# Attention scores of two heads in one product of 128 rows, in three rounded parts

## The chip, the cores and the metric

The kernel runs on one core of one Trainium2 chip. What counts is the device time of one execution in microseconds (us), as the median of several runs. The engines work side by side, each through its own instructions in order: TensorE (PE in the rows; its weight loads are PEld), VectorE (DVE), ScalarE (ACT), GpSimd (POOL), and SyncE (SP), which only issues DMAs here.

## What is computed

The reference is a trunk of two layers over 256 tokens of width 1024. In each layer one projection of the normalised input feeds three token mixers: attention with a window of 128 tokens (8 query heads, 2 key heads of 64), a state space branch (S5 with a gated linear unit), and a convolution branch. Their outputs are gated, added and projected onto the residual; a SwiGLU feed-forward block and a gated per-layer embedding follow. The attention scores, which the change touches:

```python
scores = jnp.einsum('bnqkgd,bnjkd->bnkgqj', qb, kb) * (HEAD_DIM ** -0.5)
scores = jnp.where(mask[None, :, None, None], scores, NEG_INF)
m = jnp.maximum(jnp.max(scores, axis=-1, keepdims=True), sink)
pr = jnp.exp(scores - m)
denom = jnp.sum(pr, axis=-1, keepdims=True) + jnp.exp(sink - m)
```

`qb` has 4 query heads (g) for each of 2 key heads (k). All data are float32.

## The kernel before, in words

The 256 tokens are two blocks of 128 (t = 0, 1), which lie on the 128 partitions. Every large matrix product is made by `gemm` (L443): a weight pair of 128 x 1024 is loaded by SyncE, split by ScalarE into a rounded part `wh` (L176, the type float32r) and by VectorE into the rest `wl` (L200), and each product of a float32 matrix is three TensorE products of rounded parts: high x high, high x low, low x high. A buffer of `wh` or `wl` comes free when TensorE has used it, so the splits follow TensorE's pace. `split` (L229) is the helper: a ScalarE copy for the high part, a VectorE subtraction for the low part (with a factor: a scaled copy and one multiply-and-subtract).

The products of a layer stand in a list, `ORDER` (L34): `zk`, `zc`, `zq` project to keys and values with the state space input, convolution input, and queries; `g..` are the gates, `y.` the attention's output projection, `c.` the convolution's, `u.` the gated linear unit's four pieces (u0 and u1 make the left half of the merged tensor `M`, u2 and u3 the right half). Then come `mo` (the mix's output), `fz` and `fo` (feed-forward), `ez` and `pz` (embedding).

Everything else runs as streams, Python generators that are advanced by `pump` (L387) after every six products of a `gemm`. A stream gives its next instructions when a model of the engines' clocks says that their inputs are there; for VectorE, ScalarE and POOL only up to a certain time ahead of TensorE's clock (5.5 us in layer 0's mix, 3.9 in layer 1's). So the order on every engine is fixed when the program is built, by modelled times, and each engine takes it in that order. Streams with a smaller number go first: attention 2, set-up of the state space branch (`ssm_prep`) 3, state space (`ssm_stream`) and convolution (`conv_stream`) 4. In layer 0 `ssm_prep` runs beside the mix: a long chain on POOL, then on VectorE, ScalarE and TensorE, and its last pieces (`kt`, `TJ`) are inputs of the state space branch (`yx`).

`attn_stream` (L830) handles one block: it turns the rotated keys and queries with TensorE (`kTp`, `qTp`), copies them with ScalarE to `kT` (L843) and `qT` (L849, with the factor 0.125), and makes the scores in one or two batches (one of eight heads for block 0, whose window holds 128 keys; two of four heads for block 1 with 256). A batch fills two PSUM banks. In each bank a rounded product with the identity writes the mask (L861), then plain float32 products of 64 rows add the scores (L864): bank 0 takes the heads of key head 0, whose 64 rows are the upper half of the partitions, bank 1 those of key head 1 in the lower half. VectorE takes the row maxima (L871), ScalarE the exponentials (L879). The products with the values (`po`) and the turn back (`oT`) follow. In the profile the tile of the scores is `sc`.

Of the kernel before, what the change touches and what calls it, by code (L numbers as in the profile page):

```python
# [6 lines left out]
F32 = mybir.dt.float32  # L7
F32R = mybir.dt.float32r
# [22 lines left out]
GELU_C = 0.7978845608028654  # L31
GELU_A = 0.044715

ORDER = ["zk zc zq g20 g10 g11 g00 g21 g01 y0 y1 c0 c1 u0 u2 u1 u3".split(),  # L34
         "zk zq zc g01 g11 g10 g00 y0 u0 g20 y1 c0 u2 u1 g21 c1 u3".split()]
AHEAD = 3
NBUF = 4
# [37 lines left out]
def bc(ap, axis, n):  # L75
    a = ap.unsqueeze(axis)
    shape = list(a.shape)
    shape[axis] = n
    return a.broadcast_to(shape)


def trunk_kernel(tc, wts, par, bmat, cst_d, x_d, pos_d, pt_d, bias_d, fg_d, out_d, dbg=None):
# [3 lines left out]
    with ctx:  # L86
# [8 lines left out]
        def b2(shape, dt=F32, name="b2"):  # L95
            return act.tile(shape, dt, tag="b2", bufs=25, name=name)
# [76 lines left out]
        def copy(out, in_, scale=None):  # L173
            if scale is None:
                run("act", 80 + 0.833 * cols(out), [out], [in_])
                ACT.copy(out=out, in_=in_)  # L176
            else:
                func(out, in_, AF.Copy, scale)
# [81 lines left out]
        POOL.memset(mhalf, -0.5)  # L260
        POOL.memset(phalf, 0.5)
        POOL.memset(one1, 1.0)
        mone = cp.tile([128, 8], F32, name="mone")
        POOL.memset(mone, -1.0)
        brow = [cp.tile([128, 512], F32, name=f"brow{i}") for i in range(3)]
# [562 lines left out]
            tt(z2, ra[:, 2], ra[:, 3], ALU.add)  # L828

        def attn_stream(t, S):  # L830
            zqk, vt, kT, par_l = S["zqk"], S["vt"], S["kT"], S["par"]
            nk = 128 * (t + 1)
            hpt = 1024 // nk
            mk = maskr[:, 256 - nk:256]
            z = zqk[t]
            yield lambda: S["rope_ok"]
            yield on_dve(z)
            rope_step(t, z)
            yield on_pe(z)
            zf = z.rearrange("p h d -> p (h d)")  # L840
            pt = p_tr("kTp")
            transpose(pt[:, 0:128], zf[:, 512:640])
            copy(kT[:, 128 * t:128 * t + 128], pt[:, 0:128])  # L843
            S["k_done"] += 1
            pt = p_tr("qTp")
            for k in range(4):
                transpose(pt[:, k * 128:k * 128 + 128], zf[:, k * 128:k * 128 + 128])
            qT = b2([128, 4, 128], name="qT")
            copy(qT.rearrange("p a b -> p (a b)"), pt, 0.125)  # L849
            yield lambda: S["k_done"] > t  # L850
            st = act.tile([128, 6, 8], F32, tag="ast", bufs=4, name="ast")
            sink = par_l[:, O_SINK:O_SINK + 8]
            scs = []
            for b in range(8 // hpt):
                sc = b4([128, hpt, nk], name="sc")
                scs.append(sc)
                yield from sm_units.take(2)
                pts = [p_sm("sc").rearrange("p (i k) -> p i k", k=nk) for _ in range(2)]
                yield on_pe(qT, kT, into=pts)
                for hf in range(2):  # L860
                    mm(pts[hf], identr, bc(mk, 1, hpt // 2), True, False)  # L861
                    rows = slice(64 * hf, 64 * hf + 64)
                    for i in range(hpt // 2):
                        mm(pts[hf][:, i], qT[rows, b * hpt // 2 + i, :],  # L864
                           kT[rows, 128 - nk + 128 * t:128 * t + 128], False, i == hpt // 2 - 1)
                sl = slice(hpt * b, hpt * b + hpt)
                mx = st[:, 0, sl].rearrange("p (i f) -> p f i", f=2)
                for hf in range(2):
                    yield on_dve(pts[hf])
                    run("dve", 615, [st], [pts[hf]])  # L870
                    DVE.reduce_max(out=mx[:, hf], in_=pts[hf], axis=AX.X)  # L871
                yield on_dve(st)
                tt(st[:, 1, sl], st[:, 0, sl], sink[:, sl], ALU.max)
                tt(st[:, 2, sl], sink[:, sl], st[:, 1, sl], ALU.subtract)
                ts(st[:, 1, sl], st[:, 1, sl], -1.0, ALU.mult)
                for i in range(hpt):
                    yield on_act(st)
                    slot = hpt * b + i
                    func(sc[:, i], pts[i % 2][:, i // 2], AF.Exp, bias=st[:, 1, slot:slot + 1],  # L879
                         accum_out=st[:, 4, slot:slot + 1])  # L880
                sm_units.give(2)
            yield on_act(st)
            func(st[:, 3, :], st[:, 2, :], AF.Exp)
            yield on_dve(st)
            tt(st[:, 4, :], st[:, 4, :], st[:, 3, :], ALU.add)
            recip(st[:, 5, :], st[:, 4, :])
            pTs = {}
            for g in range(2):
                for kb in range(t + 1):
                    yield on_pe(*scs)  # L890
                    pt = p_tr("pT")
                    for i in range(4):
                        slot = 4 * g + i
                        transpose(pt[:, i * 128:i * 128 + 128],
                                  scs[slot // hpt][:, slot % hpt, kb * 128:kb * 128 + 128])
                    pT = b2([128, 4, 128], name="pTs")
                    copy(pT.rearrange("p h q -> p (h q)"), pt)
                    pTs[g, kb] = pT
            yield from sm_units.take(1)
            po = p_sm("po")  # L900
            yield on_pe(*pTs.values(), into=[po])
            for g in range(2):
                for i in range(4):
                    slot = 4 * g + i
                    kv = slot % 2
                    for kb in range(t + 1):
                        mm(po[:, slot * 64:slot * 64 + 64], pTs[g, kb][:, i, :], vt[kb][:, kv * 64:kv * 64 + 64],
                           kb == 0, kb == t)
            o = b2([128, 8, 64], name="o")
            yield on_dve(po, st)  # L910
            tt(o, po.rearrange("p (h d) -> p h d", h=8), bc(st[:, 5, :], 2, 64), ALU.mult)
            sm_units.give(1)
            yield on_pe(o)
            of = o.rearrange("p h d -> p (h d)")
            pt = p_tr("oT")
            for k in range(4):
                transpose(pt[:, k * 128:k * 128 + 128], of[:, k * 128:k * 128 + 128])
            hi, lo = b2([128, 4, 128], F32R, name="aTh"), b2([128, 4, 128], F32R, name="aTl")
            split(hi.rearrange("p a b -> p (a b)"), lo.rearrange("p a b -> p (a b)"), pt)
            S["aT"][t] = (hi, lo)  # L920
# [154 lines left out]
        def layer(l, feat, sts, prep):  # L1075
# [4 lines left out]
            hrstd = [stat(sts, 5, t) for t in range(NT)]  # L1080
            S["zqk"] = [act.tile([128, 10, 64], F32, tag="zqk", bufs=2, name="zqk") for t in range(NT)]
            S["vt"] = [act.tile([128, 128], F32, tag="vt", bufs=2, name="vt") for t in range(NT)]
            S["kT"] = act.tile([128, 256], F32, tag="kT", bufs=1, name="kT")
            S["Ux"] = Ux = b2([128, 8, 64], name="Ux")

            def e_zk(acc):
# [37 lines left out]
            rows = {}  # L1124
# [507 lines left out]
```

## Time and profile before

| | before |
|---|---|
| median of 3 runs | 831.92 us (831.0 to 832.2) |
| profiled execution | 831.12 us, span 829.3 us |
| TensorE busy | 813.3 us (98%) |
| weight loads | 674.4 us (81%) |
| VectorE busy | 572.3 us (69%) |
| ScalarE busy | 479.2 us (58%) |
| POOL busy | 127.4 us (15%) |
| DMA | mean 176 GB/s, 58.6% of the DMA engines' time |
| granted TensorE clock | full, 0.997 on average |

The span is the time from the first to the last instruction; 1.8 us of the execution lie outside it. Busy TensorE time counts the modelled ends of pipelined products, so that what one product costs is read from the distance between starts, or from a long piece divided by its count. In the chain of waits, the profile goes back from the last instruction, at each step to what released it or to the instruction before it on the same engine; what stands in the chain set the end of the execution.

### The profile page before, as it was taken

To read this page: it belongs to the slowest core of one execution; us is meant where nothing else is said; L and a number is where in the kernel's file an instruction comes from. 1 tells how busy PE (TensorE), PEld (TensorE's weight loads), DVE (VectorE), ACT (ScalarE), POOL (GpSimd) and SP (SyncE) were. 2 spreads that over 40 slices of the span, in tenths; PEclk is the share of its full clock that TensorE was granted. 3 is DMA by queue.
4 is the path that set the end of the run, shared out by engine and by line. 5 is a ranking of instruction groups with operands and counts; after the bars stand their busy time and mean duration, and the time that the engine had idled before them with its cause. 6 is when DMAs were issued, how large, how long until landed. Compare 5 with 4: busy or idle time off the path is not lost.

```text
span 829.3 us, 11031 instructions
## 1 busy us (share of the span) xinstructions
PE 813.3 (98%) x3920; PEld 674.4 (81%) x3920; DVE 572.3 (69%) x864; ACT 479.2 (58%) x779; POOL 127.4 (15%) x314
## 2 busy tenths in 40 slices
PE   8999999899999999999999999999999999999996
PEld 7787898778887888888888878888888888888885
DVE  4689887695676876554578589877765666664555
ACT  6776865565546665553674575566555445444354
POOL 5889002000837000000110000100010000000011
PEclk9999999999999999999999999999999999999998
DMA  8765443457656655666555444667666666665662
GB/s 257 240 195 165 140 128 101 149 165 216 184 176 180 179 177 158 191 182 197 182 157 163 152 141 127 202 208 218 170 204 180 187 185 184 182 198 179 199 180 79
DMA packets 43687, 146.35 MB, mean 176 GB/s; under 512 B 4976, under 2 KB 6384, under 8 KB 43632
## 3 DMA queue, kind: packets, MB, share of 16 engines
q1 hardware_dynamic: 43632, 145.65, 58.6%
q8 instruction: 31, 0.51, 0.3%
q14 instruction: 24, 0.20, 0.1%
HBM read 144.58 MB, written 1.05 MB: 176 GB/s over the span
## 4 chain that ended last, share of the span: by engine, by line
PE 88%; DVE 4%; ACT 3%; DMA 3%; issue 1%; SPq 0%; POOLq 0%; POOL 0%; ACTq 0%; DVEq 0%
PE fz L227 27%; PE g L227 14%; PE fo L227 14%; PE mo L227 5%; PE pz L227 4%; PE u L227 3%; DMA raw<-in_wts 3%; PE zq L227 3%; PE sc L227 2%; PE ya L227 2%; DVE wl L200 2%; PE pl L227 1%; PE ez L227 1%; PE zk L227 1%; PE yx L227 1%; PE po L227 1%
## 5 line engine op out<-in xcount | busy, mean ns | idle before, releaser
L200 DVE TENSOR_TENSOR wl<-raw,wh 128x1024 fp32r<-128x1024 f32 (+1 forms) x261 | 316.4, 1215 | 201.9 <-ACT wh L176 201.6
L176 ACT CAST wh<-raw 128x1024 fp32r<-128x1024 f32 (+1 forms) x261 | 272.5, 1046 | 183.2 <-PE fo L227 57.1
L200 POOL TENSOR_TENSOR nst<-nst 128x2 f32<-128x2 f32 (+1 forms) x14 | 2.8, 200 | 498.9 <-ACT sqj L171 498.4
L227 PE MATMUL fz<-wh,f0h 128*128 128x512 f32 x176 | 70.1, 399 | 0.0
L227 PE MATMUL fz<-wh,f1h 128*128 128x512 f32 x176 | 69.6, 395 | 0.0
L227 PE MATMUL fo<-wh,hdh 128*128 128x512 f32 x176 | 68.8, 391 | 0.0
L227 PE MATMUL fz<-wh,f0l 128*128 128x512 f32 x176 | 68.7, 390 | 0.0
L227 PE MATMUL fz<-wh,f1l 128*128 128x512 f32 x176 | 68.6, 390 | 0.0
L227 PE MATMUL fz<-wl,f0h 128*128 128x512 f32 x176 | 68.6, 390 | 0.0
L227 PE MATMUL fz<-wl,f1h 128*128 128x512 f32 x176 | 68.6, 390 | 0.0
L227 PE MATMUL fo<-wh,hdl 128*128 128x512 f32 x176 | 68.5, 389 | 0.0
L227 PE MATMUL fo<-wl,hdh 128*128 128x512 f32 x176 | 68.5, 389 | 0.0
L227 PE MATMUL g<-wh,h0h 128*128 128x512 f32 x96 | 38.9, 405 | 0.0
L227 PEld LDWEIGHTS fz<-wh,f0l 128*128 128x128 f32 x176 | 33.0, 188 | 7.1
L227 PEld LDWEIGHTS fz<-wh,f1l 128*128 128x128 f32 x176 | 33.0, 188 | 7.0
L227 PEld LDWEIGHTS fo<-wh,hdl 128*128 128x128 f32 x176 | 33.0, 188 | 6.9
L227 PE MATMUL g<-wh,h1h 128*128 128x512 f32 x96 | 38.5, 401 | 0.0
L227 PEld LDWEIGHTS fo<-wh,hdh 128*128 128x128 f32 x176 | 33.1, 188 | 6.7
L227 PEld LDWEIGHTS fo<-wl,hdh 128*128 128x128 f32 x176 | 33.1, 188 | 6.7
L227 PEld LDWEIGHTS fz<-wl,f1h 128*128 128x128 f32 x176 | 33.1, 188 | 6.5
L227 PEld LDWEIGHTS fz<-wh,f1h 128*128 128x128 f32 x176 | 33.1, 188 | 6.5
L227 PEld LDWEIGHTS fz<-wl,f0h 128*128 128x128 f32 x176 | 33.1, 188 | 6.4
(374 smaller groups left out, 1749.3 us busy)
## 6 DMA issues: line engine op xcount, KB each, us to landing
raw<-in_wts SPq DMA_DIRECT2D x258, 512.0 KB, 3.6
brow<-in_bias SPq DMA_DIRECT2D x20, 256.0 KB, 4.0
raw<-in_wts SPq DMA_DIRECT2D x4, 256.0 KB, 4.1
out<-e SPq DMA_DIRECT2D x4, 256.0 KB, 2.2
x<-in_x SPq DMA_DIRECT2D x4, 128.0 KB, 3.9
x<-in_x SPq DMA_DIRECT2D x2, 256.0 KB, 4.9
bm<-in_bmat SPq DMA_DIRECT2D x4, 128.0 KB, 4.8
pT<-in_pt SPq DMA_DIRECT2D x2, 256.0 KB, 4.5
```

What stands on the lines that cost most here:

```text
L176: ACT.copy(out=out, in_=in_)
L200: (eng or DVE).tensor_tensor(out=out, in0=a, in1=b, op=op)
L227: PE.matmul(out, lhsT, rhs, start=start, stop=stop, skip_group_check=onto)
```

## The change

The scores of two heads are made by one product over all 128 rows. The keys of a layer are kept in `kz`: for each of the two key heads a copy of all 128 rows in which the other head's 64 rows are zero, side by side, so that a product of the turned queries of a head pair (one from each key head) with `kz` gives both heads' scores next to each other: 256 columns in block 0, 512 in block 1. Keys and queries are no longer plain float32; each is split into two rounded parts, and a product becomes three: high x high, high x low, low x high. The zeros come from a factor per partition (`pick`, ones and zeros, set by four memsets on POOL at the start). The heads of a batch go to the banks in pairs, so the maxima are written side by side and the exponentials read another bank for the same head. `kz` and the second query tile are taken from the tag `b2`. In layer 0's order u1 and u2 change places.

```diff
-ORDER = ["zk zc zq g20 g10 g11 g00 g21 g01 y0 y1 c0 c1 u0 u2 u1 u3".split(),
+ORDER = ["zk zc zq g20 g10 g11 g00 g21 g01 y0 y1 c0 c1 u0 u1 u2 u3".split(),
...
+        pick = [pows[:, 5 + g:6 + g] for g in range(2)]
+        for g in range(2):
+            for h in range(2):
+                POOL.memset(pick[g][64 * h:64 * h + 64], 1.0 if g == h else 0.0)
...
-            copy(kT[:, 128 * t:128 * t + 128], pt[:, 0:128])
+            for g in range(2):
+                split(kz[0][:, g, 128 * t:128 * t + 128], kz[1][:, g, 128 * t:128 * t + 128], pt[:, 0:128], pick[g])
...
-            qT = b2([128, 4, 128], name="qT")
-            copy(qT.rearrange("p a b -> p (a b)"), pt, 0.125)
+            qT = [b2([128, 4, 128], F32R, name=f"qT{i}") for i in range(2)]
+            split(*[w.rearrange("p a b -> p (a b)") for w in qT], pt, 0.125)
...
-                yield on_pe(qT, kT, into=pts)
+                yield on_pe(*qT, *kz, into=pts)
+                n = hpt // 2
                 for hf in range(2):
-                    mm(pts[hf], identr, bc(mk, 1, hpt // 2), True, False)
-                    rows = slice(64 * hf, 64 * hf + 64)
-                    for i in range(hpt // 2):
-                        mm(pts[hf][:, i], qT[rows, b * hpt // 2 + i, :],
-                           kT[rows, 128 - nk + 128 * t:128 * t + 128], False, i == hpt // 2 - 1)
+                    mm(pts[hf], identr, bc(mk, 1, n), True, False)
+                    for i in range(n // 2):
+                        c = (hpt * b + n * hf) // 2 + i
+                        o = pts[hf][:, 2 * i:2 * i + 2]
+                        for x, y in ((0, 0), (0, 1), (1, 0)):
+                            mm(o, qT[x][:, c, :], kz[y][:, :, 0:nk], False, x == 1 and i == n // 2 - 1)
                 sl = slice(hpt * b, hpt * b + hpt)
-                mx = st[:, 0, sl].rearrange("p (i f) -> p f i", f=2)
                 for hf in range(2):
                     yield on_dve(pts[hf])
                     run("dve", 615, [st], [pts[hf]])
-                    DVE.reduce_max(out=mx[:, hf], in_=pts[hf], axis=AX.X)
+                    DVE.reduce_max(out=st[:, 0, hpt * b + n * hf:hpt * b + n * hf + n], in_=pts[hf], axis=AX.X)
...
-                    func(sc[:, i], pts[i % 2][:, i // 2], AF.Exp, bias=st[:, 1, slot:slot + 1],
+                    func(sc[:, i], pts[i // n][:, i % n], AF.Exp, bias=st[:, 1, slot:slot + 1],
...
-            S["kT"] = act.tile([128, 256], F32, tag="kT", bufs=1, name="kT")
+            S["kz"] = [b2([128, 2, 256], F32R, name="kz") for i in range(2)]
```

## Rows read from the trace of the kernel before

**Rows 1.** The page: busy time of TensorE, and the chain's shares by engine.
```profile
PE 813.3 (98%) x3920; PEld 674.4 (81%) x3920; DVE 572.3 (69%) x864; ACT 479.2 (58%) x779; POOL 127.4 (15%) x314
...
PE 88%; DVE 4%; ACT 3%; DMA 3%; issue 1%; SPq 0%; POOLq 0%; POOL 0%; ACTq 0%; DVEq 0%
```

**Rows 2.** Busy us of each engine in stretches (xinstructions), granted clock, DMA share, GB/s.
```profile
76.00:100.00 24.00, 24.00 (x109) 18.46 (x108) 20.42 (x38) 17.45 (x36) 6.50 (x11) 1.00 0.51 153
100.00:117.00 17.00, 17.00 (x117) 15.36 (x116) 15.42 (x33) 12.28 (x26) 0.00 (x0) 1.00 0.43 125
117.00:140.00 23.00, 22.85 (x137) 19.81 (x136) 21.90 (x33) 11.03 (x18) 3.81 (x3) 1.00 0.31 92
140.00:168.00 28.00, 24.61 (x133) 19.91 (x132) 17.23 (x26) 17.86 (x33) 1.70 (x6) 1.00 0.53 163
...
454.00:530.00 76.00, 75.94 (x407) 62.92 (x407) 62.12 (x128) 44.98 (x90) 0.00 (x0) 1.00 0.49 146
```

**Rows 3.** Timeline of TensorE in layer 0: start, us, instruction, [idle before, and releaser].
```profile
157.62 0.50 PE L227 MATMUL yc<-wh,cTh 128*128 128x512 f32 x1 [1.18 <-ACT cTh L171]
...
176.99 0.50 PE L227 MATMUL u<-wh,sTh 128*128 128x512 f32 x1 [1.18 <-ACT u L171]
```

**Rows 4.** The chain that ended last, in order of time (start, us, what), 117 to 207.
```profile
119.05 1.23 DVE wl L200
...
137.96 0.44 PE kt L277 x2
```

**Rows 5.** The same chain: pieces of the scores, and one of `ya`.
```profile
63.63 2.88 PE sc L227 x18
...
77.66 2.79 PE sc L227 x10
...
139.79 5.44 PE ya L227 x24
...
468.67 2.83 PE sc L227 x18
```

**Rows 6.** Timeline near the end: rounded products of 256 columns and a weight load.
```profile
817.29 0.28 PE L227 MATMUL pl<-wh,p1h 128*128 128x256 f32 x1
817.29 0.19 PEld L227 LDWEIGHTS pl<-wl,p1h 128*128 128x128 f32 x1
817.41 0.28 PE L227 MATMUL pl<-wl,p1h 128*128 128x256 f32 x1
```

**Rows 7.** Timeline of TensorE: the turn of the keys; products behind layer 0's scores.
```profile
60.14 0.27 PE L277 MATMUL kTp<-cst,zqk 128*128 128x128 f32 x1
...
80.38 0.50 PE L227 MATMUL g<-wh,h0h 128*128 128x512 f32 x1
80.71 0.40 PE L227 MATMUL g<-wl,h0h 128*128 128x512 f32 x1
```

**Rows 8.** Timeline of VectorE in layer 0: a split's lower part, and operations of 128 columns.
```profile
110.84 0.69 DVE L200 TENSOR_TENSOR aTl<-oT,aTh 128x512 fp32r<-128x512 f32 x1
111.45 0.88 DVE L210 SCALAR_TENSOR_TENSOR cacc<-ubuf,cst,cacc 128x256 f32<-128x256 f32 x2
...
115.26 1.24 DVE L210 SCALAR_TENSOR_TENSOR cperm<-ubuf,cst,cacc 128x128 f32<-128x128 f32 x4
```

**Rows 9.** Timeline of VectorE: the first and the last of four waits in layer 0.
```profile
86.42 1.23 DVE L200 TENSOR_TENSOR wl<-raw,wh 128x1024 fp32r<-128x1024 f32 x1 [1.15 <-ACT wh L176]
...
93.96 1.23 DVE L200 TENSOR_TENSOR wl<-raw,wh 128x1024 fp32r<-128x1024 f32 x1 [0.66 <-ACT wh L176]
```

**Rows 10.** Timeline of ScalarE in layer 1: the copy of the keys.
```profile
461.73 0.25 ACT L176 COPY kT<-kTp 128x128 f32<-128x128 f32 x1
```

**Rows 11.** Timeline of POOL at the start.
```profile
0.78 0.10 POOL L262 MEMSET pows<- 128x1 f32 x1
...
7.68 0.19 POOL L189 CAST posf<-pos 128x2 f32<-128x2 int32 x1 [3.20 <-DMA raw<-in_wts]
```

**Rows 12.** Timeline of VectorE in layer 1, just ahead of its scores.
```profile
463.44 1.23 DVE L200 TENSOR_TENSOR wl<-raw,wh 128x1024 fp32r<-128x1024 f32 x1 [4.02 <-ACT wh L176]
```

More of the change, by code (lines that the diff above doesn't have):

```diff
@@ L830, in attn_stream @@
         def attn_stream(t, S):
-            zqk, vt, kT, par_l = S["zqk"], S["vt"], S["kT"], S["par"]
+            zqk, vt, kz, par_l = S["zqk"], S["vt"], S["kz"], S["par"]
             nk = 128 * (t + 1)
```

## Prediction

> **What bounds the kernel now.** I read the page first [rows 1]: TensorE is busy for 813.3 of 829.3 us, and 88% of the chain that ended last is TensorE. A busy TensorE is not yet a bound, since the ends of its products are modelled, so I read the stretches next [rows 2]. In layer 1's mixing stage (454 to 530 us) TensorE works 75.94 of 76 us and VectorE 62.12: time taken off TensorE there is time taken off the end. Layer 0 is different. From 117 to 140 us TensorE and VectorE are both full (22.85 and 21.90 of 23 us), and from 140 to 168 TensorE stands still for 3.4 of 28 us. That is four waits in the timeline, with a fifth of 1.18 us to follow at 176.99, 4.6 us together; [rows 3] shows the first and the last of the five, and each ends on a ScalarE or VectorE instruction. The chain of waits says the same: from 119 to 138 us it runs along VectorE (weight split, set-up of the state space branch, its scan) and comes back to TensorE with `kt` at 137.96 [rows 4]. So the two layers are costed apart: TensorE decides in layer 1; in layer 0 TensorE and VectorE run neck and neck and VectorE decides at the end. After layer 0's mix, TensorE is the chain almost without a break.
>
> **The products of the scores.** This is what the change removes, and it lies on TensorE in both layers. The chain has three pieces named `sc` in each layer, one for token block 0 and two for block 1 [rows 5]: 2.88 and 2.83 us for block 0, and four of 2.79 or a little less for block 1; together 5.71 + 4 x 2.79 = 16.9 us. Each holds two mask products and eight (block 0) or four (block 1) products of 64 rows in plain float32, which the trace shows as two instructions each.
> Afterwards block 0 has two mask products and twelve products of 256 columns in the rounded type, block 1 twice two masks and six products of 512 columns. The trace has both forms: 24 products of 512 columns take 5.44 us in `ya`, 0.227 each [rows 5], and two 256-column products of `pl` start 0.12 us apart [rows 6]. That gives 2 x 0.227 + 12 x 0.12 = 1.89 for block 0 and 8 x 0.227 = 1.82 for each half of block 1, 5.53 us a layer, 11.1 in all: 5.8 us less.
> A smaller term goes with it. The first rounded product behind float32 products takes longer: from 80.38 to the next start at 80.71 is 0.33 instead of 0.227 [rows 7]. It happens behind four groups of block 1, 0.4 us. Behind block 0 stand float32 transposes, so nothing goes there. TensorE work falls by 6.2 us, 3.1 a layer.
>
> The 256-column products each have weights of their own, and in [rows 6] such a load (0.19 us as recorded) begins with the product before it and costs nothing on top of the 0.12. "TensorE: Matmul & The Clock Gate" of the Trainium skill, section "Part 3: Packing small matmuls — row/col tiling", says that a weight load overlaps products in flight only where its row group differs; here all would be whole-array. The same page's LDWEIGHTS section gives a load of 128 columns as about 107 ns; by an estimate from it, 24 new products a layer with the load in the open would cost 2.6 us more, and 0.5 us of the 3.1 would be left. The rows speak against that, and I keep the sum; the open load is a small rival below, priced there from rows.
>
> **VectorE: two splits more.** Keys and queries were written by one ScalarE copy each. Now each is split, and the lower part is VectorE's. Of a split of 512 columns VectorE holds 0.61 us (`aTl` at 110.84, next start 111.45), of a 128-column operation with a factor from a tile 1.24 / 4 = 0.31 [rows 8]. A stream (one token block of one layer) adds one of the former and two of the latter: 1.23 us, 2.46 a layer, on an engine that takes its work in order. What waits behind them in layer 0 is the convolution's accumulation and the set-up of the state space branch.
> In layer 1 this is hidden: VectorE has 13.9 us free in 454 to 530 [rows 2]. In layer 0 it is open. Between 76 and 100 us VectorE is idle for 3.6 us, mostly in waits for ScalarE's half of a weight split (four of them, [rows 9] has the first and the last), and these are paced by TensorE, which frees the buffers. Extra work put down around 60 to 68 us can vanish in those 3.6 us; but a TensorE that is ahead by some 2 us closes part of the same gaps. The bounds for layer 0's end are thus: all of TensorE's 3.1 us is kept (VectorE's work vanishes in the gaps), or none and VectorE's 2.46 us come on top (the chain of [rows 4] starts that much later). The waits of 84 to 97 us are nearest to where the extra work lies and could hold all of it, while the full stretch of 117 to 140 us gives nothing back; I take a gain of 1.1 us, a little above the middle (-3.1 and +2.46 have -0.3 between them) because the gaps come first.
>
> **ScalarE, POOL, order.** ScalarE copies the keys twice instead of once: 0.25 us for one [rows 10], perhaps 0.35 with the factor, up to 0.45 a stream. It is idle for 6.6 of the 24 us from 76 to 100 [rows 2], and the copy ends up in the latency of the scores, which start 3.5 us after the transpose of the keys anyway (60.14 in [rows 7] to 63.63 in [rows 5]); nothing. If that cover is gone it costs 0.9 us a layer, inside the layer's bounds. POOL gets four single-column memsets of 0.10 us as recorded, ahead of a 3.20 us wait for the positions [rows 11]: nothing; uncovered 0.4 us at most. Loads and queues stay as they are: the gated linear unit's weights come in another order, as many as before.
> The order u0, u1, u2, u3 brings the left half of the merged tensor to its end one piece earlier, so its transposes and splits come before the third piece's results rather than after them. That moves work, it removes none; the stall of 1.18 us at 176.99 [rows 3], where an accumulator is seeded behind such a split on ScalarE, can go, or come at the next seed as well. I take zero, with 1.2 us to either side.
> The maxima and the exponentials have the same sizes; only which bank holds which head changes.
>
> **The sum.** -3.1 (layer 1) - 1.1 (layer 0) = -4.2 us. The profiled execution lasted 831.12 us, 1.8 of it outside the span, 0.8 below the median of 831.92. I take the 4.2 off the profiled span (829.3 to 825.1) and give the forecast against the median: 827.7 us.
>
> **The rivals.**
> *Layer 0 keeps it all.* The gaps of VectorE swallow the 2.46 us and the waits of [rows 3] move with TensorE. For it: the gaps come before the full stretch. Against it: five stalls that end on other engines. -6.2 us: 825.7, and 824.5 if the order takes the 1.18 away too.
> *VectorE decides layer 0.* The extra work is not absorbed; the chain of [rows 4] starts between 0 and 2.46 us late. -3.1 + 0 to 2.46: 828.8 to 831.3.
> *Slower: TensorE waits for the lower parts.* The scores now need an instruction from VectorE's queue, where before ScalarE's copy was enough. The place of the scores in TensorE's order is planned with modelled times; where VectorE really stands behind a wait for a weight split (4.02 us at 463.44, just where layer 1's scores are made ready [rows 12]), TensorE stops with its whole queue. It is paid once a stream, four times. From 1.55 us a stream the 6.2 us are gone; at 4.0 each the kernel would be 9.8 us slower, 841.7. Against it: several microseconds lie between the transposes and the scores now, and TensorE's five stalls in the mix all come much later.
> *Loads in the open.* If a whole-array product had to wait for its weights, each of the 24 new products of a layer would take up to the recorded load of 0.19 us [rows 6] more: 4.6 us a layer, 9.1 in all, and -6.2 + 9.1 = 2.9 us slower, 834.8. It decides from 0.13 us a product. The 0.12 from start to start in the same rows speaks plainly against it.
>
> **How the numbers follow.** Forecast 0.43; layer 0 keeps it all 0.20; VectorE decides 0.25; slower by waiting 0.10; loads in the open 0.02. About 0.2% (1.7 us, below 830.3) is what a measurement of this kernel can tell from no change. Faster: 0.43 + 0.20 + half of 0.25 = 0.755, said as 0.75. Same: the other half of VectorE's case, 0.13. Slower: 0.10 + 0.02 = 0.12. The range takes in the first three cases with the order's bound: 824.5 to 831.4.
>
> **What would show it.** Right: `sc` pieces of about 1.9 us, three a layer; TensorE free of waits on the scores; layer 1's mix some 3 us shorter; the five stalls of layer 0 longer in sum by about 2 us. Wrong: steps of 0.2 us or more between the 256-column products; a TensorE wait that names `kz` or `qT` and VectorE; `kt`, `yc` or the first `u` of layer 0 at the same time as before or later, which is the second rival; or layer 1's gain coming back as a new wait.

## The result, and the profile after

| | before | after |
|---|---|---|
| median | 831.5 us (831.0 to 832.2, 4 runs) | 837.46 us (836.85 to 838.15, 4 runs) |
| ratio | | 1.0071, 95% interval 1.0057 to 1.0085 |
| profiled execution | 831.12 us, span 829.3 | 837.26 us, span 835.2 |

The change makes the kernel 6 us slower. The prediction said 827.7 us, faster than before; the time lies above its range (824.5 to 831.4). In what follows, "the kernel before" in a batch of experiments is its median in that batch, 830.98 to 831.52 us.

The page of after, the lines that answer to [rows 1]:

```profile
PE 812.2 (97%) x3904; PEld 676.9 (81%) x3904; DVE 577.2 (69%) x876; ACT 480.1 (57%) x783; POOL 125.9 (15%) x318
...
PE 85%; DVE 5%; ACT 5%; DMA 2%; issue 1%; POOL 0%; SPq 0%; POOLq 0%; ACTq 0%; DVEq 0%
```

VectorE has 4.9 us more work, which is the 2 x 2.46 of the prediction. TensorE's share of the chain fell from 88 to 85%, and VectorE's and ScalarE's rose: somewhere TensorE now waits for them. The stretches, to be read against [rows 2] (the columns are the same; 462 to 538 us is layer 1's mixing stage, which begins later than before; the clock is the third number from the end):

```profile
117.00:140.00 23.00, 23.00 (x158) 20.87 (x157) 19.35 (x31) 11.41 (x17) 3.08 (x4) 1.00 0.37 110
140.00:168.00 28.00, 21.23 (x119) 18.03 (x118) 20.07 (x32) 12.86 (x28) 3.14 (x4) 0.88 0.38 117
168.00:212.00 44.00, 39.19 (x173) 31.90 (x173) 30.12 (x51) 25.30 (x42) 0.00 (x0) 0.88 0.46 134
462.00:538.00 76.00, 75.49 (x411) 64.36 (x410) 66.05 (x136) 47.33 (x93) 0.00 (x0) 1.00 0.51 153
```

Layer 1 is as full as it was. Layer 0 from 140 to 212 us is not: TensorE stands still for 6.8 of 28 us instead of 3.4, then for 4.8 of 44 instead of 1.2, and the granted clock is 0.88, where before it was 1.00. The last stretch before:

```profile
168.00:212.00 44.00, 42.82 (x205) 35.31 (x204) 34.52 (x58) 27.56 (x48) 5.08 (x14) 1.00 0.62 186
```

The chain of waits of after (start, us, what) shows where the time goes:

```profile
72.88 1.88 PE sc L227 x14
...
93.67 1.84 PE sc L227 x8
...
103.24 1.85 PE sc L227 x8
...
129.36 1.38 PE ya L227 x6
...
157.87 0.43 PE kt L281 x2
158.30 4.70 PE yc L227 x18
163.00 5.32 PE yx L227 x48
...
172.42 1.10 PE sT L281 x4
...
212.66 1.36 PE fz L227 x6
...
491.09 1.84 PE sc L227 x8
```

And two pieces of the same chain of the kernel before, for the ends of the stage, with a row of TensorE's timeline between them:

```profile
145.24 5.32 PE yx L227 x48
...
150.74 0.48 PE L227 MATMUL ya<-wh,aTh 128*128 128x512 f32 x1
...
204.10 1.36 PE fz L227 x6
```

First, the scores. Their pieces are 1.88 and 1.84 us, as the prediction said (1.89 and 1.82), instead of 2.88 and 2.79 [rows 5]. Second, their place. They begin at 72.7 us instead of 63.5. Third, the rest of layer 0: the last `kt`, with which the set-up of the state space branch ends, comes at 157.87 instead of 137.96 [rows 4], and `yx` at 163.0 instead of 145.2. The products of the attention's output (`ya`) stood in two pieces before: ahead of `yx` (139.79, [rows 5]) and behind it (from 150.74), between the second turn of the convolution (`cT`) and the convolution's output products (`yc`, 157.62, [rows 3]). In after they begin at 129 and are used up at 147, ahead of that turn; `yc` then comes ahead of `yx`, and behind `yx` nothing is left to do while ScalarE and VectorE work on its result. Layer 0 ends (first `fz`) 8.56 us later. From there to the end of the span it is 622.5 us, before 625.2: layer 1 gives 2.7 back. The sum is +5.9 us.

What TensorE waited for from 55 to 215 us in after (us in total, times, longest):

```profile
PE sT L281 <- DVE gtm L214: 4.1, 1, 4.1
PE cT L281 <- ACT cn L171: 3.5, 1, 3.5
PE yc L227 <- ACT cTh L171: 3.2, 1, 3.2
PE u L227 <- ACT sTh L171: 0.7, 1, 0.7
PE qTp L281 <- DVE qT L210: 0.5, 1, 0.5
```

That is 12.0 us in place of 4.7 before (the five stalls of the prediction, 4.6, and one of 0.2 at `kt`), 7.3 more, and none of it at a product of the scores. Behind the wait of 3.2, products of 512 columns start 0.42 us apart instead of 0.23, as these rows of TensorE's timeline show:

```profile
154.95 0.79 PE L227 MATMUL yc<-wh,cTh 128*128 128x512 f32 x1 [3.22 <-ACT cTh L171]
155.54 0.63 PE L227 MATMUL yc<-wl,cTh 128*128 128x512 f32 x1
155.96 0.63 PE L227 MATMUL yc<-wh,cTl 128*128 128x512 f32 x1
```

### The profile page after: what moved, and what is told of

It reads as the page before. It is cut to its first block, busy times and chain, and to the rows that moved or that the text cites. A ratio compares the mean times of both kernels' runs of the same rounds, so it can differ in the third digit from the quotient of the medians.

```text
span 835.2 us, 11024 instructions
## 1 busy us (share of the span) xinstructions
PE 812.2 (97%) x3904; PEld 676.9 (81%) x3904; DVE 577.2 (69%) x876; ACT 480.1 (57%) x783; POOL 125.9 (15%) x318
## 4 chain that ended last, share of the span: by engine, by line
PE 85%; DVE 5%; ACT 5%; DMA 2%; issue 1%; POOL 0%; SPq 0%; POOLq 0%; ACTq 0%; DVEq 0%
PE fz L227 27%; PE fo L227 14%; PE g L227 13%; PE mo L227 5%; PE pz L227 4%; PE u L227 3%; DMA raw<-in_wts 2%; DVE wl L200 2%; PE yc L227 2%; PE ya L227 1%; ACT wh L176 1%; PE pl L227 1%; PE zq L227 1%; PE ez L227 1%; PE zk L227 1%
## 5 line engine op out<-in xcount | busy, mean ns | idle before, releaser
L227 PE MATMUL fz<-wh,f0h 128*128 128x512 f32 x176 | 70.1, 398 | 0.0
L227 PEld LDWEIGHTS fz<-wh,f0h 128*128 128x128 f32 x176 | 33.1, 188 | 6.3
```

The costliest lines, as they stand in the source:

```text
L227: PE.matmul(out, lhsT, rhs, start=start, stop=stop, skip_group_check=onto)
```

## The experiments

Two questions were put. Does the loss come from the change's own instructions (too much work on VectorE in layer 0, or scores that come late), or from the order in which the rest of layer 0 now stands on the engines? An operation does two things in this kernel: it takes time on its engine, and its charge to the modelled clock moves what is planned after it. (The first runs were made to try the lateness of keys and scores, alone or with VectorE's work, which their expectations call theory A and its variants; the order came in as a theory of its own only after the run with the dummy operations.)

### The order of the gated linear unit's pieces

```diff
-ORDER = ["zk zc zq g20 g10 g11 g00 g21 g01 y0 y1 c0 c1 u0 u1 u2 u3".split(),
+ORDER = ["zk zc zq g20 g10 g11 g00 g21 g01 y0 y1 c0 c1 u0 u2 u1 u3".split(),
```

> The change with layer 0's old order of the linear unit's pieces (u0, u2, u1, u3), nothing else. In the changed kernel layer 0's mix ends 8.6 us later than before (first product of the feed-forward block at 212.7 instead of 204.1 us) and layer 1 gives 2.7 back. Theory A, late scores: the lower parts stand in VectorE's queue, block 0's scores wait for block 1's keys too, the attention comes 9 to 16 us later and pushes the set-up of the state space branch back; the order plays no part: 837.5 within 1. Rival B, the amount: VectorE's 2.46 us more are enough by themselves: the same, 837.5. Rival C, the order moves the pieces into a worse place: 829 to 832.

Measured 838.29 us, ratio 1.0090 [1.0073, 1.0107]; the scores start at the same time as in after (72.6 us), and the same three stalls stand in the same places. The exchange of u1 and u2 is not the cause: without it the kernel is no faster; the medians differ by 0.8 us, and the two intervals overlap.

### The change in layer 1 alone

```diff
-            S["attn"] = [Stream(attn_stream(t, S), PRI["attn"]) for t in range(NT)]
+            S["attn"] = [Stream((attn_stream if l in (1,) else attn_old)(t, S), PRI["attn"]) for t in range(NT)]
```

`attn_old` is the stream of the kernel before; the order of the pieces is the old one too.

> The new scores in layer 1 alone; layer 0 has the old scores, the old tiles and the old order. All theories that put the loss into layer 0's mix: 831.5 - 2.7 = 828.8 within 0.7, layer 0 with its times of before. If something that reaches over both layers costs the time (tiles of the shared tag, the state of the engines): 831 or more.

Measured 828.45 us, 0.9971 [0.9952, 0.9989]: 2.6 us gained, near the 3.1 of the sum. The products' term is right and layer 1 keeps most of it. The loss arises in layer 0. The kept trace is of one of the two longest of ten executions (832.32 us; eight lie between 827.67 and 828.78): in it the clock is at half from 66.0 to 72.8 us, behind a wait of 1.40 at the old scores, and layer 0 ends 3.7 us late. From there to the end of the span it too has 622.8 us, where the kernel before has 625.4 by the same rows.

### Lower parts without VectorE

```diff
-                split(kz[0][:, g, 128 * t:128 * t + 128], kz[1][:, g, 128 * t:128 * t + 128], pt[:, 0:128], pick[g])
+                for i in range(2):
+                    copy(kz[i][:, g, 128 * t:128 * t + 128], pt[:, 0:128], pick[g])
...
-            split(*[w.rearrange("p a b -> p (a b)") for w in qT], pt, 0.125)
+            for w in qT:
+                copy(w.rearrange("p a b -> p (a b)"), pt, 0.125)
```

> The change, but the lower parts of keys and queries are written by ScalarE as second rounded copies of the same data (they hold the upper part again, so the scores are not those of the reference); VectorE's 2.46 us a layer are gone and nothing of the scores stands in its queue, while all products are those of the change. A (late scores) and B (amount): layer 0's loss goes, the scores of block 0 start some 5 us earlier than in the change: 831.5 - 2.7 and up to 3.1 more, 825.5 to 829. C (order) or the products themselves: 835 or more.

Measured 828.45 us, 0.9966 [0.9953, 0.9979]. This kernel leaves out the true lower parts. With ScalarE in VectorE's place the loss is gone, though layer 0 gains nothing: the first `fz` starts at 204.4 (203.9 before), `yx` at 149.0 (145.1 before), and the first scores at 70.1, 2.6 us earlier than in after where some 5 were expected. So the loss hangs on the lower parts on VectorE. But this run changes three things at once: VectorE's work, the time at which keys are ready, and the charges, and so the order.

### Keys by blocks, upper parts first, and both

In after, `kz` holds the two blocks' keys of one head side by side, and block 0's scores are planned behind block 1's keys as well. Also, ScalarE and VectorE take turns at the two heads. This is the timeline of after at the first keys:

```profile
62.87 0.37 ACT L171 ACTIVATE kz<-kTp,pows 128x128 fp32r<-128x128 f32 x1
64.70 0.35 DVE L210 SCALAR_TENSOR_TENSOR kz<-kTp,pows,kz 128x128 fp32r<-128x128 f32 x1
65.08 0.37 ACT L171 ACTIVATE kz<-kTp,pows 128x128 fp32r<-128x128 f32 x1 [1.84 <-DVE kz L210]
...
71.24 0.34 DVE L210 SCALAR_TENSOR_TENSOR kz<-kTp,pows,kz 128x128 fp32r<-128x128 f32 x1
71.61 0.37 ACT L171 ACTIVATE kz<-kTp,pows 128x128 fp32r<-128x128 f32 x1 [3.52 <-DVE kz L210]
...
72.50 0.69 DVE L210 SCALAR_TENSOR_TENSOR qT<-qTp,qT 128x512 fp32r<-128x512 f32 x1
72.72 0.39 PE L227 MATMUL sc<-maskr,identr 128*128 128x512 f32 x1
```

ScalarE's second copy waits until VectorE has made the first head's lower part, 1.84 us in block 0 and 3.52 in block 1, and the scores start right behind the last of block 1's parts. Two edits take these away, one at a time and together:

```diff
-            S["kz"] = [b2([128, 2, 256], F32R, name="kz") for i in range(2)]
+            S["kz"] = [b2([128, 2, 2, 128], F32R, name="kz") for i in range(2)]
...
-                yield on_pe(*qT, *kz, into=pts)
+                yield on_pe(*qT, *[w[:, 0:t + 1] for w in kz], into=pts)
```

This one stores the keys block by block. The other makes both upper parts first:

```diff
             for g in range(2):
-                split(kz[0][:, g, 128 * t:128 * t + 128], kz[1][:, g, 128 * t:128 * t + 128], pt[:, 0:128], pick[g])
+                copy(kz[0][:, g, 128 * t:128 * t + 128], pt[:, 0:128], pick[g])
+            for g in range(2):
+                stt(kz[1][:, g, 128 * t:128 * t + 128], pt[:, 0:128], pick[g], kz[0][:, g, 128 * t:128 * t + 128].bitcast(F32), ALU.mult, ALU.subtract)
```

By blocks alone:

> The change with the keys stored block by block, so that block 0's scores are placed behind block 0's keys alone; upper and lower parts are written in turn as in the change. A1 (behind block 1's keys): scores at 65 to 68 us, layer 0's mix no longer than before, 825 to 830. A2 (ScalarE and VectorE wait for each other): the later pieces of the attention stay late, 832 to 838.

Upper parts first alone:

> The change with both upper parts of the keys written before the two lower ones; the storage of the keys as in the change. In the changed kernel ScalarE waits 7.3 us in four places for VectorE between the two copies of a block's keys, and VectorE 4.4 us for ScalarE. A1 (block 0's scores are late because they stand behind block 1's keys in TensorE's order): this order stays, scores at 70 to 73 us, 835 to 838. A2 (they are late because ScalarE and VectorE wait for each other): scores at 66 to 68, 825 to 830.

Both:

> The change with the keys stored block by block (each token block's two 128-column copies together), so that block 0's scores need block 0's keys alone, and with both upper parts of the keys written before the lower ones, so that ScalarE doesn't wait for VectorE between them. VectorE's work is the same in amount. A (late scores): block 0's scores start at 66 to 68 us instead of 72.7, the attention runs ahead of the set-up as before, layer 0 ends no later than before: 825.5 to 830. B (amount): VectorE has as much to do, layer 0 stays 5 us or more behind: 834 or more.

| | measured, us | ratio | first `sc` | last `kt` | `yx` | `sT` |
|---|---|---|---|---|---|---|
| after | 837.46 | 1.0071 [1.0057, 1.0085] | 72.7 | 157.7 | 162.8 | 172.4 |
| keys by blocks | 838.84 | 1.0104 [1.0070, 1.0138] | 65.9 | 140.8 | 156.8 | 177.0 |
| upper parts first | 836.06 | 1.0062 [1.0047, 1.0077] | 72.3 | 157.4 | 162.1 | 171.7 |
| both | 824.36 | 0.9922 [0.9908, 0.9937] | 66.9 | 135.6 | 142.8 | 156.7 |

Keys by blocks brings the first scores 7 us forward, and block 1's last ones to 92.5 us (before 92.8, in after 104.0), and gains nothing: late scores alone are not the cause. Upper parts first, with the same list as after on TensorE, is not clear of it (the intervals overlap). Both together beat after by 13 us and the kernel before by 6.7 us. The times of keys by blocks and of both lie outside what any theory had said, by 0.8 us above and 1.1 below. VectorE has the same 876 operations in all four (577.2 us in after, 575.3 with both). The amount of work on VectorE cannot explain 838.84 beside 824.36. What differs is where the planned work of layer 0 stands, and how ScalarE and VectorE wait for each other at the keys.

### What the low clock costs

```diff
+            if S is S0:
+                fill(cpt, 16)
```

The same stands ahead of `yc` with 14 and ahead of `sT` with 18 products, in the changed kernel; `fill` puts that many unread products of 512 columns into a bank that is about to be written.

> The change, with 48 products more in layer 0 that nobody reads, put into TensorE's order where it stands still in the changed kernel: 16 ahead of the second turn of the convolution, 14 ahead of its first output product, 18 ahead of the turn of the state space output. They fill the three stalls of 3.8, 3.5 and 4.4 us with 0.227 us a product and write banks that are written anew behind them. In the changed kernel the granted clock is 0.5 for 6.8 and 10.2 us behind these stalls, and 10 products of yc and 13 of u start 0.427 apart instead of 0.227. If the lower clock costs its own time: it stays full, 23 x 0.2 = 4.6 us less, 833. If the next wait takes the time back (the chain runs on VectorE and ScalarE anyway): 836 to 838.

Measured 833.1 us, 1.0024 [1.0015, 1.0034], 4.4 us less than after. Three stretches of after show the clock (the third number from the end: 1.00, 0.50 and 0.57):

```profile
147.00:151.00 4.00, 0.74 (x5) 0.37 (x3) 3.90 (x7) 0.33 (x1) 3.14 (x4) 1.00 0.57 186
...
155.00:159.00 4.00, 4.00 (x11) 3.08 (x12) 2.53 (x3) 1.48 (x3) 0.00 (x0) 0.50 0.20 42
...
168.00:180.00 12.00, 7.19 (x21) 5.39 (x21) 4.49 (x7) 5.16 (x9) 0.00 (x0) 0.57 0.24 77
```

and the same stretches with the stalls filled:

```profile
147.00:151.00 4.00, 4.00 (x21) 3.21 (x20) 3.76 (x6) 0.56 (x1) 2.80 (x4) 1.00 0.60 192
...
155.00:159.00 4.00, 4.00 (x19) 3.21 (x19) 2.92 (x5) 2.59 (x10) 0.00 (x0) 1.00 0.36 105
...
168.00:180.00 12.00, 11.31 (x52) 8.61 (x51) 8.71 (x20) 8.71 (x16) 0.00 (x0) 1.00 0.22 63
```

TensorE's waits are filled here, not removed. In after TensorE comes out of them at half the clock and starts 11 products from 155 to 159 us, where it starts 19 at the full one. So some 4.4 us of the loss are the clock's (by the two ratios 3.9), and the stalls are the rest. The Trainium skill, "TensorE: Matmul & The Clock Gate", section "Part 1: The HAM clock gate", gives the two levels as 1.2 and 2.4 GHz and 427 and 216 ns between starts of 512 columns. The rows agree at half the clock, 0.42 us; at the full one they have 0.227, 5% more.

### Amount or order: work without charge, charge without work

These three tell the two theories apart on the kernel before, with its old scores. First, VectorE's extra operations of the change, into tiles that nothing reads, charged like all others:

```diff
             copy(kT[:, 128 * t:128 * t + 128], pt[:, 0:128])
+            for g in range(2):
+                stt(S["kd"][:, g, 128 * t:128 * t + 128], pt[:, 0:128], phalf[:, 0:1], kT[:, 128 * t:128 * t + 128], ALU.mult, ALU.subtract)
...
+            stt(qd.rearrange("p a b -> p (a b)"), pt, 0.125, qT.rearrange("p a b -> p (a b)"), ALU.mult, ALU.subtract)
```

> The kernel before with VectorE's additional work of the change and nothing else: per block and layer two operations of 128 columns and one of 512 that write tiles which nobody reads (one tile of the shared tag a layer, one a stream); the scores are the old ones and don't wait for them. Theory A (lateness): the scores keep their place; what is left is 2.46 us of work: 831 to 833.5. Rival B (amount): layer 0 loses its 8.6 us, or much of it, without any new score: 835 to 840.

Measured 850.24 us, 1.0214 [1.0186, 1.0243]. The scores keep their place (62.5 us, before 63.5), and nothing reads the extra tiles; still the kernel loses 19 us, 3 times as much as the change does and far above what either theory had said. Taken by itself this looks like a full VectorE. Next, the same operations, issued to VectorE directly, so that the model is not charged (the two calls of `stt` become calls of `DVE.scalar_tensor_tensor` with the same operands):

```diff
-                stt(S["kd"][:, g, 128 * t:128 * t + 128], pt[:, 0:128], phalf[:, 0:1], kT[:, 128 * t:128 * t + 128], ALU.mult, ALU.subtract)
+                DVE.scalar_tensor_tensor(out=S["kd"][:, g, 128 * t:128 * t + 128], in0=pt[:, 0:128], scalar=phalf[:, 0:1],
+                                         in1=kT[:, 128 * t:128 * t + 128], op0=ALU.mult, op1=ALU.subtract)
```

> The kernel before with the lower parts computed by VectorE into tiles that nothing reads, as in the run with the dummy splits (850.24 us), but without charging them in the costs by which the kernel orders its own work: every engine's list of work is that of the kernel before, with twelve more instructions for VectorE, 4.9 us in all. Theory 'amount' (VectorE lacks the time in layer 0): as the charged dummies, 845 to 850 us, sT in layer 0 late by some 15 us. Theory 'order' (what is lost is lost by the order that the charge leads to): 831 to 834 us, sT within 3 us of the kernel before's 163.0, no long stall of TensorE added.

And the charge alone, with no operation behind it:

```diff
+            for g in range(2):
+                run("dve", 80 + 1.04 * 128 + 60, [], [pt[:, 0:128], kT[:, 128 * t:128 * t + 128]])
...
+            run("dve", 80 + 1.04 * 512, [], [pt, qT])
```

> The kernel before with the lower parts charged in the costs by which the kernel orders its work, but not computed: TensorE's list is exactly that of the run with the dummy splits (850.24 us), and VectorE has no instruction more than in the kernel before. Theory 'order': 842 to 850 us, sT in layer 0 at 178 to 183 us with the stalls and the half clock of the dummy run. Theory 'amount': 831 to 834 us, sT near 163.

| the kernel before with | measured, us | ratio | TensorE waits, 55 to 215 us (before: 4.7) | first `fz` (before: 203.9) |
|---|---|---|---|---|
| work and charge | 850.24 | 1.0214 [1.0186, 1.0243] | 13.3 | 222.4 |
| work, no charge | 831.81 | 1.0008 [0.9999, 1.0018] | 4.9 | 204.2 |
| charge, no work | 850.37 | 1.0234 [1.0210, 1.0259] | 12.0 | 221.4 |

In the whole execution, TensorE, ScalarE and GpSimd have the lists of the kernel before in the second run, and in the third those of the first, instruction for instruction; VectorE's lists differ in the twelve operations alone. The 4.9 us of work, with the extra tiles that they write, cost 0.8 us or nothing. The charge, with no work behind it, costs 19.3. The chain of the run with the charge alone shows how:

```profile
123.90 1.22 DVE v L200 x2
...
129.80 2.25 DVE sw L218 x2
132.05 1.20 DVE v L200 x2
...
146.74 0.42 PE kt L277 x2
...
157.65 0.64 ACT cTh L171
158.33 2.93 PE yc L227 x6
161.26 10.13 PE yx L227 x48
...
221.55 1.36 PE fz L227 x6
```

Before, the six operations `v` of the set-up stand in one piece on VectorE (120.28, 121.51 and 123.44 in its chain) ahead of the state space branch's `sw` and its scan. Here three of them stand before the scan and three behind it, at 132.05. They feed the copy `CAi` (134.2 us instead of 124.2), four groups of `kt` (from 135.7 instead of 125.8) and with them the last `kt` (146.74 instead of 137.96). Then the convolution's turn and normalisation, and `sT`, each stand alone, with nothing left for TensorE to do meanwhile:

```profile
PE yc L227 <- ACT cTh L171: 5.3, 1, 5.3
PE sT L277 <- DVE gtm L214: 4.2, 1, 4.2
PE kt L277 <- DVE ks L200: 1.8, 1, 1.8
```

Two of them are waits of after: `yc` for `cTh` and `sT` for `gtm`. `yx`, at 161.26, runs at half the clock, 10.13 us for what takes 5.32. The split of the `v` is not what after has: there all six stand ahead of the scan, but the first begins at 127.93 instead of 120.19.

What the lists share is the place of `ya`. Laid side by side, TensorE's lists fall into two groups. In the kernel before, layer 1 alone, ScalarE's lower parts, both key edits together and the three runs with uncharged work, `yx` stands ahead of `yc`, with `ya` left behind it; these take 824.4 to 833.5 us. In after, the old order of pieces, keys by blocks, upper parts first, the dummy operations and the charge alone, `ya` is used up ahead of the convolution's second turn and `yc` begins ahead of `yx`; these take 836.1 to 850.4 us (the run with the filled stalls, which has after's list, 833.1). That this place costs the time is read from these lists; no run moved it alone.

### The change without the charges

The change itself, its operations in the same sequence, with only the lower parts not charged:

```diff
-                split(kz[0][:, g, 128 * t:128 * t + 128], kz[1][:, g, 128 * t:128 * t + 128], pt[:, 0:128], pick[g])
+                hi, lo = [w[:, g, 128 * t:128 * t + 128] for w in kz]
+                copy(hi, pt[:, 0:128], pick[g])
+                DVE.scalar_tensor_tensor(out=lo, in0=pt[:, 0:128], scalar=pick[g], in1=hi.bitcast(F32), op0=ALU.mult, op1=ALU.subtract)
```

The queries' split likewise.

> The changed kernel with every instruction and product of the change, the lower parts on VectorE in the same alternating sequence of splits, but these not charged in the costs by which the kernel orders its work (12 instructions uncharged), so that scores and what follows are ordered as if the copies by ScalarE alone stood ahead of them. Theory 'order': layer 0 keeps part of the gain, sT at 158 to 166 us, 824 to 831 us. Theory 'amount' or 'late keys' (the alternating splits themselves make the scores late): as the change, 835 to 840 us, with TensorE waiting 5 us or more at the first scores, where the changed kernel has other work placed.

Measured 833.46 us, 1.0024 [1.0013, 1.0035]: 4.0 us better than after, 2.5 outside what the theory of the order said. `sT` stands at 165.4, and the long waits for `cn` and `gtm` are gone. But a wait has come that after does not have, at the first scores, now placed early:

```profile
66.35 0.50 PE L227 MATMUL sc<-kz,qT 128*128 128x256 f32 x2 [3.48 <-ACT qT L171]
```

The queries' copy stood on ScalarE behind the second key copy, and this one waited for VectorE. So the same with both upper key parts first, TensorE's list unchanged:

```diff
+            for g in range(2):
+                copy(kz[0][:, g, 128 * t:128 * t + 128], pt[:, 0:128], pick[g])
             for g in range(2):
                 hi, lo = [w[:, g, 128 * t:128 * t + 128] for w in kz]
-                copy(hi, pt[:, 0:128], pick[g])
                 DVE.scalar_tensor_tensor(out=lo, in0=pt[:, 0:128], scalar=pick[g], in1=hi.bitcast(F32), op0=ALU.mult, op1=ALU.subtract)
```

> The run with uncharged lower parts (833.46 us) with both upper key copies ahead of both lower ones, in place of one head's pair after the other's; TensorE's list is the same instruction for instruction. It tells what the 3.5 us wait for the eight transposed queries at the first scores, and the half clock behind it, come from. Theory 'alternation' (ScalarE's second key copy waits for VectorE's first lower part, and the copy of the queries behind it): the wait falls below 1 us, no half clock near 79 us, 826 to 830 us. Theory 'queue' (the lower parts stand behind a weight split in VectorE's queue, whatever ScalarE does): the query copy is early, but the products that read the lower parts wait in its place, 2 to 3.5 us, and the time stays at 831.5 to 834 us.

Measured 829.15 us, 0.9971 [0.9955, 0.9987]: 4.3 us better again, and faster than the kernel before. Its waits at the first scores:

```profile
64.44 0.39 PE L227 MATMUL sc<-kz,qT 128*128 128x256 f32 x1 [0.51 <-ACT qT L171]
...
65.75 0.39 PE L227 MATMUL sc<-kz,qT 128*128 128x256 f32 x1 [0.93 <-DVE kz L851]
...
66.35 0.74 PE L227 MATMUL sc<-kz,qT 128*128 128x256 f32 x4 [0.21 <-DVE qT L859]
```

1.65 us are left of 3.7: 0.51 that end on ScalarE's copy and 1.14 on VectorE. Neither theory had this run whole: the time is that of "alternation", the wait lies between the two (below 1 us was said by the one, 2 to 3.5 by the other), and the half clock behind the first scores, which "alternation" said would go, is still there. It stands at some 67.3 to 70.7 us in the traces of both uncharged runs of the change (the expectation put it near 79). This trace is of an execution of 830.6 us with a mean clock of 0.994; four of the ten had 0.998 and took 827.25 to 829.12. Beside the run with the same parts in the same sequence, but charged (836.06), the missing charge is worth 6.9 us.

## Why the prediction was wrong

**The scores' products: right.** 1.88 and 1.84 us a piece, 1.89 and 1.82 said. The weight loads of the 256-column products stay hidden, as [rows 6] had it: six such products with loads of their own take 0.87 us, the last one's 0.28 included, which is 0.12 from start to start. The rival of loads in the open did not come.

```profile
72.94 0.87 PE L227 MATMUL sc<-kz,qT 128*128 128x256 f32 x6
```

**Layer 1: right, a little large.** 3.1 us said, 2.7 in the two traces, 2.6 by the run with layer 1 alone.

**VectorE's amount: right in kind, and it never mattered.** The prediction put 2.46 us a layer between vanishing and costing in full. The work without its charge costs 0.8 us over both layers (interval -0.1 to 1.5). That fits the argument that the gaps of [rows 9] come first; in which gaps the work went was not followed.

**Layer 0: the step that failed.** It is the sentence "The bounds for layer 0's end are thus: all of TensorE's 3.1 us is kept [...], or none and VectorE's 2.46 us come on top". Both bounds treat the rest of layer 0 as a list that stays as it is and is shifted. The kernel's own description says that the list is made from modelled clocks, and that VectorE's operations are given out only a limited time ahead of TensorE's. Six operations a layer that are charged to VectorE's clock change that list. This was priced at nothing, without a reason: of order, the prediction weighed u1 and u2 alone. Measured, the first `fz` came 8.56 us late, not 1.1 early; in the new list `ya` is used up ahead of `cT`, and `yx` stands last. Worked out from the rows: 7.3 us more of stalls, 4.4 us of low clock (the filled run), less the 3.1 of the products, 8.6. So VectorE did not decide layer 0's end by its load, as the prediction had it; the planned order did.

**The slower rival: its place was right, its weight not.** "TensorE waits for the lower parts" does not occur in after at a score: no wait of a `sc` product stands in its list. That is because the scores were planned behind the parts, at 72.7 us. The sign named for it shows only in small, where the turn of block 1's queries (`qTp`) waits for VectorE's `qT`, 0.5 us in layer 0 and 0.3 in layer 1. Where the plan puts them early, the wait comes, 3.5 us at the first scores in the run without charges, more than the 1.55 a stream from which the prediction let it decide, though only once. It went over ScalarE, which the prediction had costed at nothing, or 0.9 us a layer uncovered: the second key copy waits for VectorE, and the queries' copy behind it. Taking turns cost 4.3 us without charges (833.46 to 829.15); with charges the medians differ by 1.4 (837.46 to 836.06), within the intervals.

**The five stalls.** They were to become longer by 2 us. In their place came five of 12.0 us in all, of which only the one of `yc` for `cTh` stood there before (1.2 us, now 3.2). The clock fell among them, which the prediction did not consider at all: the clock of layer 0's mix was 1.00 in every row it read.

**"Layer 0 keeps it all"** was given 825.7 us and 0.20. The version with keys by blocks and upper parts first shows that it can be had: 824.36 us, the first `fz` at 200.28, 3.8 us earlier than before, with every product and split of the change:

```profile
67.04 1.88 PE sc L227 x14
...
200.28 1.36 PE fz L227 x6
```

**What stays open.** That the charge moves the order, and that the order costs the time, is shown on the kernel before. On the change the missing charge is worth 4.0 and 6.9 us, by the two uncharged runs of the change, in which the scores are also planned at other times. In the second of these layer 0 still ends at 207.20, 3.1 us later than before, with three waits of `u` for ScalarE (3.7 us together) and the clock at half for 3.4 us twice; these were not taken apart. Why the charges put half of `v` behind the scan, or bring `ya` ahead of the turn, was not followed through the model; that VectorE's clock then runs against the limit ahead of TensorE's is argued only. And the gain of "both" over its two halves (824.36 beside 838.84 and 836.06) shows how far a list can jump; that this one is no more than a lucky list is not excluded.

## What to carry to other kernels

Where a kernel plans its own order from modelled costs, an added operation has two prices, its time and its charge, and the second can be far the larger (here 19.3 us beside 0.8 or nothing): before costing such an edit, ask what would be planned differently, and try the charge without the work and the work without the charge. Take a dummy run for a measure of an engine's room only if the order of all other work is the same instruction for instruction. When one engine makes the upper and the other the lower part, try making all upper parts first, so that no copy stands between two engines that wait for each other; here it was worth 4.3 us in one pair of runs and nothing clear of noise in another.

## What was not expected of the hardware

The granted clock of TensorE fell to half inside a layer that ran at 1.00 before: in after at 152.6 us, within the second of two waits of 3.5 and 3.2 us, and again at 169.6, within one of 4.1. Products of 512 columns then started 0.42 us apart instead of 0.227, and `yx` took 10.13 us for 5.32 in the run with the charge alone. In after this came to 4.4 us, more than the whole gain of the cheaper scores in a layer. Short waits were followed by it as well: in the trace of layer 1 alone a single one of 1.40 us (half from 66.0 to 72.8), in that of the uncharged change with upper parts first 0.51 and 0.93 with one product between them (67.3 to 70.7). The unread products that kept the clock up cost nothing that shows, since TensorE would have stood still in their place; what they cost by themselves was not measured.
